# Native products of 8 columns ahead of streams, and odd heads of the scan on the other half of the rows

## The chip, the cores and the metric

The kernel runs on one core of one Trainium2 chip. The metric is the device time of one execution in microseconds (us); shorter is better. One program covers the whole computation: two layers of a network on 256 tokens of width 2048, in f32. The engines are named as in the profile: PE (TensorE, the matrix products), PEld (PE's weight loads), DVE (VectorE), ACT (ScalarE), POOL (GpSimd) and SP (SyncE, which here only issues transfers); ACTq is the queue on which ACT issues instructions such as transfers.

## What is computed

Layer 0 has differential attention as its mixer, layer 1 an RWKV-7 time mix; each is followed by an FFN. Cut to what the change touches:

```python
def sqrelu_mlp(h, w1, w2):                 # w1: 2048 x 8192, w2: 8192 x 2048
    u = jax.nn.relu(h @ w1)
    return (u * u) @ w2

# diff_attention: q = h @ wq, k = h @ wk, v = h @ wv, ..., o @ wo   (each 2048 x 2048)

def rwkv7_time_mix(h, ...):                # r = xr @ wr, k = xk @ wk, v = xv @ wv
    def step(state, inp):                  # 32 heads, state 64 x 64 each, 256 steps
        rt, wt, kt, vt, kkt, at = inp
        sa = jnp.einsum('bhvk,bhk->bhv', state, -kkt)
        state = (state * wt[:, :, None, :]
                 + sa[..., None] * (kkt * at)[:, :, None, :]
                 + vt[..., None] * kt[:, :, None, :])
        yt = jnp.einsum('bhvk,bhk->bhv', state, rt)
        return state, yt
    _, y = lax.scan(step, state0, xs)
    ...
    return out @ wo
```

## The kernel before

**Products.** A weight arrives as f32 (`raw`, loaded by SP's queue) and is split in two parts of a shorter float format: `whi` (a cast on ACT, L115) and `wlo` (a subtraction on DVE, L116). The other operand is split in the same way. Each product is made of three: high by high, high by low, low by high. In the form of `mm_a` (L220 to L222) the split weights are what 512 columns of the other side are multiplied with; in `mm_bh` (L254 to L256) the moving side has 256 columns. `proj_b` runs `mm_b` over panels: a panel is 256 output columns, its two accumulators are in PSUM banks of the role "mm" or "a" in turn, and one panel is 2 x 2 x 2 calls of `mm_bh` of 4 x 3 products, that is 96.

**FFN.** Each FFN runs four blocks (`fb`), which take 32 panels of the first weight as `proj_b` in a stream of 256-column products, each block followed by a stretch of 512-column products of the second weight (`mm_a`). The first block has only 6 panels in `proj_b`, since its first two are interleaved with the work ahead; the others have 8, that is 768 products. In front of the first product of blocks 1 to 3 stands a lead, chosen by the table LEADS (L33): native f32 products of the identity by itself into a bank of the role "d", of 128, 8, 24 or 72 columns, or four of 128. In FFN1's block 2 the entry is "low": the first three products stand in another order, and no native one is put there. A product of two f32 operands, called native here, leaves two records in the trace.

**Scan.** The time mix is computed in chunks of 64 tokens for four groups of eight heads (`g`). `scan_chain` works through one group: it loads the 64 x 64 inverses `TP` (in 32-blocks, and the off-diagonal parts `T1` and `T2` that make the missing block in ps1 and ps2) from DRAM, copies v into `VU`, transposes KB into `kbt` (L1275, L1277), and then goes through four chunks `c`, in each of which `W` is copied out of PSUM (L1330), eight heads' products `pu` of 64 x 64 x 64 are made from TP and W (L1339), and copied to `VU` (L1341). All eight heads' TP of a chunk stand on the same 64 rows (partitions), `b`. The generators of the groups and of the gates, norms and projections that surround them are merged to one stream by `beside`, `tick` and `yield` (a number says how much of other work is to come between); PE's order is fixed when the program is built, with products of the v and wo weights (`mm_a`, L220 to L222) as what stands between the steps of the scan. The semaphores among engines are set by the builder. Transfers of ACT and SP signal on eight shared completion lanes (DMAHW0 to DMAHW7 in the order below).

**Places in the profile.** wq and wk run to 187 us, wv, attention and wo to 390, FFN0 to 1104, the projections of the time mix to 1400, the scan to about 1680, FFN1 to 2400.

Of the kernel before, what the change touches and what calls it, by code (L numbers as in the profile page):

```python
# [20 lines left out]
P = 128  # L21
# [9 lines left out]


LEADS = {(0, 1): 128, (0, 2): 8, (0, 3): 24, (1, 1): 72, (1, 2): "low", (1, 3): 4}  # L33
# [4 lines left out]
class Kern:  # L38
    def __init__(self, ctx, tc, a, upto):
# [29 lines left out]
        self.lead = None  # L69
# [163 lines left out]

    def mm_bh(self, ps, XH, XL, half, c, m, first, last, ks=range(4)):
# [3 lines left out]
        for k in ks:  # L238
            xh, xl = XH[c][:, k, :], XL[c][:, k, :]
            lead, self.lead = self.lead, None  # L240
            if lead == "low":
                nc.tensor.matmul(ps[m], lhsT=wl[:, k, cl], rhs=xh, start=True, stop=False)
                nc.tensor.matmul(ps[m], lhsT=wh[:, k, cl], rhs=xh, start=False, stop=False)
                e = nc.tensor.matmul(ps[m], lhsT=wh[:, k, cl], rhs=xl, start=False, stop=False)
                continue
            else:
                if lead:
                    bank = self.ps("d")
                    with self.behind(self.done):
                        for _ in range(4 if lead == 4 else 1):  # L250
                            n = P if lead == 4 else lead
                            e = nc.tensor.matmul(bank[:, :n], lhsT=self.ident, rhs=self.ident[:, :n], start=True, stop=True)
                with self.behind(*([e] if lead else [])):
                    nc.tensor.matmul(ps[m], lhsT=wh[:, k, cl], rhs=xh, start=first and k == 0, stop=False)  # L254
# [4 lines left out]
    def proj_b(self, w, XH, XL, evac, panels=range(8), roles=("mm",)):  # L259
# [170 lines left out]
    def attention(self, xs):  # L430
        nc, a, tc = self.nc, self.a, self.tc
        with ExitStack() as ctx:
# [80 lines left out]
            self.proj_b(a["wq"], XH, XL, ev_q, range(1, 8), ["mm", "a"])  # L513
# [97 lines left out]
    def ffn(self, i, xs, fin, store=None):  # L611
# [3 lines left out]
        with ExitStack() as ctx:  # L615
# [42 lines left out]
            for fb in range(4):  # L658
# [16 lines left out]
                self.lead = LEADS.get((i, fb))  # L675
                self.proj_b(w1, XH, XL, evac, range(fb * 8 + 2 * (fb == 0), fb * 8 + 8), ["mm", "a"])
# [566 lines left out]
    def scan_chain(self, g, sp, pre, v, norm, done):  # L1243
# [54 lines left out]
        for b in (64, 0):  # L1298
            nc.scalar.copy(TP[b:b + 32, :, :, 32:64], ps2[b:b + 32])
# [261 lines left out]
```

## Time and profile before

| | before |
|---|---|
| time, three runs | 2404.79, 2409.40, 2412.78 us; median 2409.4 |
| profiled execution | 2411.38 us |
| its span on the core | 2409.6 us |
| PE busy | 2371.7 us, 98% |
| DVE, ACT, POOL busy | 1586.3 (66%), 1140.2 (47%), 152.1 (6%) |
| mean granted clock of PE | 0.995 |

The profile comes from one execution, whose own time stands beside its span: 1.8 us lie around it. Sums of the prediction are made against 2411.38. PE's busy time counts overlapping matmul records once; the end of a matmul is modelled, so the pitch between starts tells more than the length of a record. "xN" at the end of a row counts records; the two of a native product count as two. In the views by windows, a number after the window's bounds is its length, and the last of the engines' columns is followed by the granted clock of PE, 1.00 at 2.4 GHz and 0.50 at 1.2 GHz.

### The profile page before, as it was taken

How to read it: one execution, taken by the hardware profiler on the slowest of the kernel's cores; microseconds unless marked ns; L12 is line 12 of the kernel's file. 1: busy time of each engine (PE TensorE's matmuls, PEld its weight loads, DVE VectorE, ACT ScalarE, POOL GpSimd, SP SyncE). 2: the span in 40 equal slices, each digit the busy share in tenths (PEclk: the TensorE clock that was granted, in tenths of full speed). 3: DMA queues.
4: the chain of work that ended last, by engine and by line, in shares of the span. 5: the costliest groups of instructions: out<-in, count | busy, mean ns of one | idle time of the engine just before them, and what ended most of it. 6: DMA issues, size and time to landing. Idle time of an engine off the chain costs nothing. (4 is left out here: it accounts for less than half of the span.)

```text
span 2409.6 us, 42367 instructions
## 1 busy us (share of the span) xinstructions
PE 2371.7 (98%) x17166; PEld 2151.6 (89%) x17166; DVE 1586.3 (66%) x2543; ACT 1140.2 (47%) x1625; POOL 152.1 (6%) x208
## 2 busy tenths in 40 slices
PE   8999999999999999999999999999999999999997
PEld 8998888989989989988999977878998998988986
DVE  6667988745655655668779965668754655655655
ACT  6434656444434434455356544554644443443443
POOL 1000000000000000000001254311000000000001
PEclk9999999999999999999999999999999999999999
DMA  8665455655555555564556773435555555555563
GB/s 289 206 202 182 144 167 173 197 194 194 193 195 193 193 192 193 193 200 142 193 182 213 252 233 122 148 95 201 184 188 195 193 193 192 188 189 191 194 199 133
DMA packets 140851, 453.00 MB, mean 188 GB/s; under 512 B 27536, under 2 KB 27792, under 8 KB 140656
## 3 DMA queue, kind: packets, MB, share of 16 engines
q1 hardware_dynamic: 120176, 424.46, 53.4%
q0 software_dynamic: 5568, 16.52, 1.9%
q10 hardware_dynamic: 14912, 9.32, 1.3%
q8 instruction: 134, 2.20, 0.4%
q14 instruction: 61, 0.50, 0.1%
HBM read 433.99 MB, written 15.20 MB: 186 GB/s over the span
## 5 line engine op out<-in xcount | busy, mean ns | idle before, releaser
L116 DVE TENSOR_TENSOR wlo<-raw,whi 128x1024 fp32r<-128x1024 f32 (+1 forms) x772 | 945.0, 1228 | 598.5 <-ACT whi L115 572.3
L115 ACT CAST whi<-raw 128x1024 fp32r<-128x1024 f32 (+1 forms) x776 | 811.1, 1048 | 674.2 <-PE ps_mm L222 219.8
L254 PE MATMUL ps_mm<-fxh,whi 128*128 128x256 f32 x1023 | 284.7, 279 | 0.0
L255 PE MATMUL ps_mm<-fxl,whi 128*128 128x256 f32 x1023 | 283.9, 278 | 0.0
L256 PE MATMUL ps_a<-fxh,wlo 128*128 128x256 f32 x1024 | 283.7, 277 | 0.0
L254 PE MATMUL ps_a<-fxh,whi 128*128 128x256 f32 x1024 | 283.7, 277 | 0.0
L255 PE MATMUL ps_a<-fxl,whi 128*128 128x256 f32 x1024 | 283.7, 277 | 0.0
L256 PE MATMUL ps_mm<-fxh,wlo 128*128 128x256 f32 x1023 | 283.5, 277 | 0.0
L221 PE MATMUL ps_mm<-wlo,uh 128*128 128x512 f32 (+1 forms) x544 | 208.3, 383 | 0.0
L222 PE MATMUL ps_mm<-whi,ul 128*128 128x512 f32 (+1 forms) x544 | 208.3, 383 | 0.0
L220 PE MATMUL ps_mm<-whi,uh 128*128 128x512 f32 (+1 forms) x544 | 208.2, 383 | 0.0
L221 PE MATMUL ps_a<-wlo,uh 128*128 128x512 f32 (+1 forms) x512 | 196.0, 383 | 0.0
L222 PE MATMUL ps_a<-whi,ul 128*128 128x512 f32 (+1 forms) x512 | 195.7, 382 | 0.0
L220 PE MATMUL ps_a<-whi,uh 128*128 128x512 f32 (+1 forms) x512 | 195.5, 382 | 0.0
L256 PEld LDWEIGHTS ps_a<-fxh,wlo 128*128 128x128 f32 x1024 | 192.7, 188 | 0.0
L256 PEld LDWEIGHTS ps_mm<-fxh,wlo 128*128 128x128 f32 x1023 | 192.6, 188 | 0.0
L254 PEld LDWEIGHTS ps_a<-fxh,whi 128*128 128x128 f32 x1024 | 192.6, 188 | 0.0
L254 PEld LDWEIGHTS ps_mm<-fxh,whi 128*128 128x128 f32 x1023 | 192.4, 188 | 0.1
L255 PEld LDWEIGHTS ps_a<-fxl,whi 128*128 128x128 f32 x1024 | 192.2, 188 | 0.0
L255 PEld LDWEIGHTS ps_mm<-fxl,whi 128*128 128x128 f32 x1023 | 192.1, 188 | 0.0
L669 ACT CAST uh<-r 128x256 fp32r<-128x256 f32 x128 | 51.9, 406 | 269.0 <-DVE r L668 269.0
L222 PEld LDWEIGHTS ps_mm<-whi,ul 128*128 128x128 f32 x544 | 102.2, 188 | 19.8
(419 smaller groups left out, 4668.9 us busy)
## 6 DMA issues: line engine op xcount, KB each, us to landing
raw<-in_ffn SPq DMA_DIRECT2D x512, 512.0 KB, 4.3
raw<-in_wk SPq DMA_DIRECT2D x32, 512.0 KB, 5.0
raw<-in_wv SPq DMA_DIRECT2D x32, 512.0 KB, 4.2
raw<-in_wo SPq DMA_DIRECT2D x32, 512.0 KB, 4.3
raw<-in_rwr SPq DMA_DIRECT2D x32, 512.0 KB, 4.7
raw<-in_rwk SPq DMA_DIRECT2D x32, 512.0 KB, 4.5
raw<-in_rwv SPq DMA_DIRECT2D x32, 512.0 KB, 4.8
raw<-in_rwo SPq DMA_DIRECT2D x32, 512.0 KB, 4.5
```

The source lines that it names most:

```text
L115: self.nc.scalar.copy(hi[:, x], src[:, x])
L116: (eng or self.nc.vector).tensor_tensor(lo[:, x], src[:, x], hi[:, x].bitcast(F32), op=ALU.subtract)
L220: nc.tensor.matmul(ps[t][:, x], lhsT=xh, rhs=wh[:, k, :], start=st, stop=False)
L221: nc.tensor.matmul(ps[t][:, x], lhsT=xh, rhs=wl[:, k, :], start=False, stop=False)
L222: e = nc.tensor.matmul(ps[t][:, x], lhsT=xl, rhs=wh[:, k, :], start=False, stop=sp)
L254: nc.tensor.matmul(ps[m], lhsT=wh[:, k, cl], rhs=xh, start=first and k == 0, stop=False)
L255: nc.tensor.matmul(ps[m], lhsT=wh[:, k, cl], rhs=xl, start=False, stop=False)
L256: e = nc.tensor.matmul(ps[m], lhsT=wl[:, k, cl], rhs=xh, start=False, stop=last and k == 3)
L669: nc.scalar.copy(UH[-1][:, m % 4, :], r)
```

## The change

**Kicks.** The table LEADS goes. A method `kick()` gives, once for each panel that is named to it, one native product of the identity by 8 columns of itself, into a bank of the role "d", ordered behind `self.done`, the last product of the unit before; the panel's first product is ordered behind it. `proj_b` takes a list `kicks` of panels and sets `self.done` for each unit. Kicks stand ahead of: panel 3 of wq; panel 3 of rwr; in each FFN panel 3 of block 0 (the second of the six there) and the first panel of blocks 1, 2 and 3. That makes ten.

**Scan.** For odd heads, TP, W and so the operands of `pu` stand on the other 64 rows than for even heads (`b1 = 64 - b`). The copies of W (L1330) and VU (L1341) become two each (`swap`), of four heads; the two copies from ps2 to TP become eight of 32 x 4 x 32 elements; the loads of TP go from four of 32 x 16 x 32 to sixteen of 32 x 4 x 32, and a tile T2, on the buffer that SD uses later, takes four more loads, so that ps2's products read odd heads' blocks on the rows where T1 stands.

```diff
-LEADS = {(0, 1): 128, (0, 2): 8, (0, 3): 24, (1, 1): 72, (1, 2): "low", (1, 3): 4}
...
+    def kick(self):
+        if not self.due:
+            return []
+        self.due = False
+        with self.behind(self.done):
+            return [self.nc.tensor.matmul(self.ps("d")[:, :8], lhsT=self.ident, rhs=self.ident[:, :8], start=True, stop=True)]
...  (mm_bh)
-            lead, self.lead = self.lead, None
-            if lead == "low":
-                nc.tensor.matmul(ps[m], lhsT=wl[:, k, cl], rhs=xh, start=True, stop=False)
-                ...
+            with self.behind(*self.kick()):
+                nc.tensor.matmul(ps[m], lhsT=wh[:, k, cl], rhs=xh, start=first and k == 0, stop=False)
...  (proj_b)
         for pn in panels:
+            self.due = pn in kicks
...
-                self.mm_b(ps, XH, XL, self.unit(w[pn, u]), 8 * u, u == 0, u == 1)
+                self.done = self.mm_b(ps, XH, XL, self.unit(w[pn, u]), 8 * u, u == 0, u == 1)
...
-            self.proj_b(a["wq"], XH, XL, ev_q, range(1, 8), ["mm", "a"])
+            self.proj_b(a["wq"], XH, XL, ev_q, range(1, 8), ["mm", "a"], [3])
-                self.proj_b(w1, XH, XL, evac, range(fb * 8 + 2 * (fb == 0), fb * 8 + 8), ["mm", "a"])
+                self.proj_b(w1, XH, XL, evac, range(fb * 8 + 2 * (fb == 0), fb * 8 + 8), ["mm", "a"],
+                            [fb * 8 + 3 * (fb == 0)])
-                self.proj_b(a["rwr"], MH, ML, ev_r, [2, 3], ["mm", "a"])
+                self.proj_b(a["rwr"], MH, ML, ev_r, [2, 3], ["mm", "a"], [3])
...  (scan_chain)
+        T2 = sp.tile([P, 4, 2, 32], F32, name="T2", tag="SD")
...
             for blk in (1, 0):
-                dst = TP[b + 32 * blk:b + 32 * blk + 32].rearrange("s h a i -> s (h a) i")[:, :, 32 * blk:32 * blk + 32]
-                nc.scalar.dma_start(dst, self.ttd[g // 2][64 * blk + r0:64 * blk + r0 + 31:2].rearrange("r s i -> s r i"))
+                for e in range(2):
+                    b1 = (64 - b if e else b) + 32 * blk
+                    for q in range(2):
+                        dst = TP[b1:b1 + 32, 4 * q + 2 * e:4 * q + 2 * e + 2].rearrange("s h a i -> s (h a) i")
+                        r1 = 64 * blk + r0 + 16 * q + 8 * e
+                        src = self.ttd[g // 2][r1:r1 + 7:2].rearrange("r s i -> s r i")
+                        nc.scalar.dma_start(dst[:, :, 32 * blk:32 * blk + 32], src)
+                        if e and blk:
+                            nc.scalar.dma_start(T2[b + 32:b + 64, 2 * q:2 * q + 2].rearrange("s h a i -> s (h a) i"), src)
...
         for b in (64, 0):
-            nc.scalar.copy(TP[b:b + 32, :, :, 32:64], ps2[b:b + 32])
+            for e in range(2):
+                b1 = 64 - b if e else b
+                x, y = (z.rearrange("p (q e i) a j -> p q e (i a) j", q=2, e=2)[:, :, e] for z in (TP, ps2))
+                for q in range(2):
+                    nc.scalar.copy(x[b1:b1 + 32, q, :, 32:64], y[b:b + 32, q])
...
+        def swap(dst, src, b, back=False):
+            for e in range(2):
+                bs, bd = b, 64 - b if e else b
+                if back:
+                    bs, bd = bd, bs
+                x, y = (z.rearrange("p (h e x) -> p h e x", e=2, x=64) for z in (dst, src))
+                nc.scalar.copy(x[bd:bd + 64, :, e, :], y[bs:bs + 64, :, e, :])
...
-            nc.scalar.copy(W[b:b + 64, :], wps[b:b + 64, :])
+            swap(W, wps, b)
...
             for h in range(8):
-                nc.tensor.matmul(pu[b:b + 64, h * 64:(h + 1) * 64], lhsT=TP[b:b + 64, hx(h), t, :],
-                                 rhs=W[b:b + 64, h * 64:(h + 1) * 64], start=True, stop=True)
-            nc.scalar.copy(VU[b:b + 64, c, :], pu[b:b + 64, :])
+                b1 = 64 - b if h % 2 else b
+                nc.tensor.matmul(pu[b1:b1 + 64, h * 64:(h + 1) * 64], lhsT=TP[b1:b1 + 64, hx(h), t, :],
+                                 rhs=W[b1:b1 + 64, h * 64:(h + 1) * 64], start=True, stop=True)
+            swap(VU[:, c, :], pu, b, True)
```

The change moves instructions at two places that the prediction speaks of. The first is PE's order where block 2 of FFN1 begins; ps_a and ps_mm are PSUM banks by role, `uh` and `ul` the split inner activations, `fxh` and `fxl` the split input of the FFN. Before:

```order
L220 MATMUL ps_a<-whi,uh 128x512
L221 MATMUL ps_a<-wlo,uh 128x512
L222 MATMUL ps_a<-whi,ul 128x512
L242 MATMUL ps_mm<-fxh_18225,wlo 128x256
L243 MATMUL ps_mm<-fxh_18225,whi 128x256
L244 MATMUL ps_mm<-fxl_18229,whi 128x256
L254 MATMUL ps_mm<-fxh_18225,whi 128x256
L255 MATMUL ps_mm<-fxl_18229,whi 128x256
L256 MATMUL ps_mm<-fxh_18225,wlo 128x256
```

And now:

```order
L218 MATMUL ps_a<-whi,uh 128x512
L219 MATMUL ps_a<-wlo,uh 128x512
L220 MATMUL ps_a<-whi,ul 128x512
L238 MATMUL ps_d<-ident 128x8
L247 MATMUL ps_mm<-fxh_18355,whi 128x256
L248 MATMUL ps_mm<-fxl_18359,whi 128x256
L249 MATMUL ps_mm<-fxh_18355,wlo 128x256
```

The natural order of the three products is back, behind one native product of 8 columns (L238).

The second is ACT's order at the loads of group 2 of the scan; TP, T (T1, T2) are loaded from ttd and tnd, `o` is the normed output, `racc` an accumulator of wo, `kbt` a transposed KB. A number at the end counts equal rows behind one another. Before:

```order
L1266 DMA TP<-ttd_11366 32x16x32 x2
L1262 DMA T_16628<-tnd_11368 32x16x32
L1266 DMA TP<-ttd_11366 32x16x32 x2
L1269 COPY VU<-v 64x512 x4
L1418 ACTIVATE o<-ps_d,vec 128x128 x4
L314 COPY racc_16551<-ps_a 128x512 x2
L115 CAST whi<-raw 128x1024
L1277 COPY kbt<-ps_d 128x384
```

And now:

```order
L113 CAST whi<-raw 128x1024 x2
L1268 DMA TP<-ttd_11370 32x4x32 x8
L1258 DMA T_16696<-tnd_11372 32x16x32
L1268 DMA TP<-ttd_11370 32x4x32 x8
L1273 COPY VU<-v 64x512 x4
L1439 ACTIVATE o<-ps_d,vec 128x128 x4
L308 COPY racc_16619<-ps_a 128x512 x2
L113 CAST whi<-raw 128x1024
L1281 COPY kbt<-ps_d 128x384
```

Five loads ahead of the copies of v into VU (four of TP, one of T1) have become sixteen of a quarter of the size and one of T1, in a row; the copies behind them stand in the same order as before. With what each of the first of these loads waits for:

```order
L1268 DMA TP<-ttd_11370 32x4x32 [waits DMAHW5_49]
L1268 DMA TP<-ttd_11370 32x4x32 [waits DMAHW6_49]
L1268 DMA TP<-ttd_11370 32x4x32 [waits DMAHW0_49]
L1268 DMA TP<-ttd_11370 32x4x32 [waits DMAHW1_49]
L1268 DMA TP<-ttd_11370 32x4x32 [waits DMAHW2_49]
L1268 DMA TP<-ttd_11370 32x4x32 [waits DMAHW4_49]
L1268 DMA TP<-ttd_11370 32x4x32 [waits DMAHW5_49]
L1268 DMA TP<-ttd_11370 32x4x32 [waits DMAHW6_49]
L1258 DMA T_16696<-tnd_11372 32x16x32 [waits DMAHW7_49]
```

Each waits for one of the eight completion lanes.

## Rows read from the trace of the kernel before

**Rows 1.** The page's first part: busy us (share of the span) and instructions by engine.

```profile
PE 2371.7 (98%) x17166; PEld 2151.6 (89%) x17166; DVE 1586.3 (66%) x2543; ACT 1140.2 (47%) x1625; POOL 152.1 (6%) x208
```

**Rows 2.** Windows, records of L254 alone: length, PE busy, PEld busy, granted clock, DMA share, GB/s.

```profile
422.39:487.90 65.51, 53.20 (x192) 36.01 (x192) 1.00 0.61 197
...
749.51:836.64 87.13, 70.74 (x256) 48.02 (x256) 1.00 0.59 194
...
1711.85:1779.87 68.02, 54.12 (x192) 36.80 (x192) 1.00 0.59 193
...
2041.29:2131.75 90.46, 71.66 (x255) 47.86 (x255) 1.00 0.56 188
```

**Rows 3.** Timeline of PE ahead of three streams: start, us, engine, line, operation [idle before].

```profile
749.37 0.28 PE L252 MATMUL ps_d<-ident 128*128 128x8 f32 x2
749.51 0.36 PE L254 MATMUL ps_mm<-fxh,whi 128*128 128x256 f32 x1
749.71 0.28 PE L255 MATMUL ps_mm<-fxl,whi 128*128 128x256 f32 x1
...
1711.59 0.51 PE L294 MATMUL ps_b<-ident,pre_y 128*128 128x128 f32 x2
...
2218.79 1.05 PE L252 MATMUL ps_d<-ident 128*128 128x128 f32 x8
2219.59 0.36 PE L254 MATMUL ps_mm<-fxh,whi 128*128 128x256 f32 x1
```

**Rows 4.** Windows, records of L254 alone, in the RWKV projections (columns as in rows 2).

```profile
1262.54:1271.02 8.48, 6.74 (x24) 4.49 (x24) 1.00 0.41 134
1271.37:1272.84 1.47, 1.20 (x4) 0.73 (x4) 1.00 0.74 223
```

**Rows 5.** Windows of the scan: length, busy us of PE, PEld, DVE, ACT, POOL, granted clock, DMA.

```profile
1346.63:1347.71 1.08, 1.08 (x34) 1.01 (x33) 0.70 (x6) 1.08 (x3) 0.00 (x0) 1.00 1.03 421
1400.00:1680.00 280.00, 274.51 (x2778) 219.70 (x2777) 187.34 (x330) 140.50 (x222) 92.14 (x111) 0.99 0.48 153
1434.38:1435.45 1.07, 1.07 (x17) 1.00 (x16) 0.62 (x2) 0.90 (x1) 0.99 (x2) 1.00 0.00 0
1465.00:1472.50 7.50, 7.50 (x50) 6.55 (x48) 2.47 (x3) 1.28 (x3) 6.89 (x12) 0.59 0.58 166
```

**Rows 6.** Timeline of ACT and its queue (ACTq), then of PE, at group 2's loads.

```profile
1530.38 0.87 ACTq L1266 DMA_DIRECT2D TP<-ttd  x2
...
1533.21 2.51 ACT L1269 COPY VU<-v 64x512 f32<-64x512 f32 x4
1535.73 1.51 ACT L1418 ACTIVATE o<-ps_d,vec 128x128 f32<-128x128 f32 x4
...
1539.73 0.48 ACT L1277 COPY kbt<-ps_d 128x384 f32<-128x384 f32 x1
...
1539.15 0.55 PE L1275 MATMUL ps_d<-ident,kb 128*128 128x128 f32 x3
```

**Rows 7.** The line that loads TP (L1266): issue ns min/median/max, and landing.

```profile
L1266 ACTq DMA_DIRECT2D TP<-ttd x16: 310/501/1150, 1414.0 to 1585.0; - x16
...
DMA to landing us min/median/max: 2.1/3.6/6.7
```

**Rows 8.** Timelines at group 0's loads: ACT's queue, then PE.

```profile
1414.03 0.85 ACTq L1266 DMA_DIRECT2D TP<-ttd  x2
...
1422.87 0.50 PE L220 MATMUL ps_a<-whi,mh 128*128 128x512 f32 x1
```

**Rows 9.** Timelines in group 3: ACT, then PE.

```profile
1602.41 1.17 ACT L1299 COPY TP<-ps_mm 32x512 f32<-32x512 f32 x2
...
1604.28 0.88 PE L1339 MATMUL ps_mm<-W,TP 64*64 64x64 f32 x12 [0.23 <-issue]
```

**Rows 10.** Timeline of ACT in group 1.

```profile
1490.04 0.48 ACT L1277 COPY kbt<-ps_d 128x384 f32<-128x384 f32 x1 [3.91 <-PE ps_d L1275]
```

**Rows 11.** Timeline of PE in the scan, at the longest of its waits there.

```profile
1462.62 0.32 PE L1328 MATMUL ps_mm<-SB,ar 128*64 128x128 f32 x1 [1.60 <-DVE SB L1356]
```

More of the change, by code (lines that the diff above doesn't have):

```diff
@@ L68, in __init__ @@
         self.side = []
-        self.lead = None
+        self.done, self.due = None, False
         nc.scalar.activation(self.small(1, "act"), self.ones[:, 0:1], AF.Exp)
@@ L239, in mm_bh @@
             xh, xl = XH[c][:, k, :], XL[c][:, k, :]
-            lead, self.lead = self.lead, None
-            if lead == "low":
-                nc.tensor.matmul(ps[m], lhsT=wl[:, k, cl], rhs=xh, start=True, stop=False)
[L243 to L254, printed above, removed]
+            with self.behind(*self.kick()):
+                nc.tensor.matmul(ps[m], lhsT=wh[:, k, cl], rhs=xh, start=first and k == 0, stop=False)
             nc.tensor.matmul(ps[m], lhsT=wh[:, k, cl], rhs=xl, start=False, stop=False)
@@ L257, in mm_bh, with proj_b @@
         return e
-    def proj_b(self, w, XH, XL, evac, panels=range(8), roles=("mm",)):
+    def proj_b(self, w, XH, XL, evac, panels=range(8), roles=("mm",), kicks=()):
         for pn in panels:
+            self.due = pn in kicks
             ps = [self.ps(roles[pn % len(roles)])[:, :S] for _ in range(2)]
             for u in range(2):
-                self.mm_b(ps, XH, XL, self.unit(w[pn, u]), 8 * u, u == 0, u == 1)
+                self.done = self.mm_b(ps, XH, XL, self.unit(w[pn, u]), 8 * u, u == 0, u == 1)
             for m in range(2):
@@ L674, in ffn @@
                         evac(m, ps0[m])
-                self.lead = LEADS.get((i, fb))
-                self.proj_b(w1, XH, XL, evac, range(fb * 8 + 2 * (fb == 0), fb * 8 + 8), ["mm", "a"])
+                self.proj_b(w1, XH, XL, evac, range(fb * 8 + 2 * (fb == 0), fb * 8 + 8), ["mm", "a"],
+                            [fb * 8 + 3 * (fb == 0)])
                 if fb == 3:
@@ L1295, in scan_chain @@
                 for b in (64, 0):
-                    nc.tensor.matmul(ps2[b:b + 32, h, ap_, :], lhsT=T1[b + 32:b + 64, h, ap_, :],
-                                     rhs=TP[b + 32:b + 64, h, ap_, 32:64], start=True, stop=True)
-        for b in (64, 0):
-            nc.scalar.copy(TP[b:b + 32, :, :, 32:64], ps2[b:b + 32])
+                    r = slice(b + 32, b + 64)
+                    x = hx(h)
+                    nc.tensor.matmul(ps2[b:b + 32, x, ap_, :], lhsT=T1[r, x, ap_, :],
+                                     rhs=T2[r, x // 4 * 2 + x % 2, ap_, :] if h % 2 else TP[r, x, ap_, 32:64],
+                                     start=True, stop=True)
+        for b in (64, 0):
+            for e in range(2):
[3 more added lines that the diff above has]
+                    nc.scalar.copy(x[b1:b1 + 32, q, :, 32:64], y[b:b + 32, q])
         W = sp.tile([P, 512], F32, name="W", tag="W")
```

## The prediction

> **What bounds the kernel now.** I read the page first: TensorE is busy for 98% of the span [rows 1], so only what shortens PE's own work, or takes from or adds to its few waits, can move the end. Two kinds of PE time bear on this change. The first is the pace of the split products of 256 columns. One line's windows over eight FFN streams show it: the same 768 products take 87.13 us in one block and 90.46 in another, and the 576 of a first block 65.51 in one layer and 68.02 in the other [rows 2]. The reader is to see two paces at the full granted clock: 87.13/768 = 113.5 ns and 90.46/768 = 117.8 ns. What stands ahead of a stream goes with the pace. Ahead of a fast block stand two native records of 8 columns [rows 3]; block 2 of FFN1, the slow one, follows its last 512-column product with no native. In the slow first block of FFN1 the records ahead are two natives as well, but spread over 1711.85 - 1711.59 = 0.26 us instead of 0.14 [rows 3]. In the RWKV projections a slow stretch of 72 products (8.48 us) turns into a fast one behind four natives: 12 products in 1.47 us, of which 0.09 is the first one's longer pitch, hence (1.47 - 0.09)/12 = 115 ns, nearer to the fast pace [rows 4]; the same happens at seven such places.
>
> The second kind is the scan. From 1400 to 1680 us PE is busy 274.5 of 280 us and ACT 140.5 [rows 5]: PE is the bound there as well, and ACT has room on the average, but not at each place.
>
> **The kicks.** Ten single products of 8 columns (two records each) are put ahead of panels, and the leads of before go. One costs 749.51 - 749.37 = 0.14 us [rows 3]. Behind a 512-column stream the first product has a longer pitch anyway; inside a running 256-column stream I add that too, 0.20 instead of 0.11 [rows 3], hence 0.23 us.
> - FFN1 block 2: 90.46 goes to 87.13, less 0.14: -3.2 us. This is the pair of streams for which the trace has the exact precedent (8 columns behind a 512-column stream, fast).
> - FFN1 block 3: its lead of four products of 128 takes 2219.59 - 2218.79 = 0.80 us [rows 3] and becomes 0.14: -0.7.
> - FFN1 block 0: 68.02 - 65.51 = 2.5 us over 576 products. The kick stands ahead of the second of six panels, so 5/6 of it may go: -2.1 + 0.23 = -1.9. It is put within a running stream, where no 8-column native has stood; the nearest rows are those of the four natives [rows 4], so I take it in full and keep 0 as the other end.
> - FFN0 block 0 and wq run at the fast pace already: +0.23 each, nothing to gain. If a native within a fast stream sets the slow pace, the loss is 4.4 ns for each product left, 480 x 4.4 = 2.1 us each. wr is mixed: 0, from -0.8 to +0.8 (192 products).
> - FFN0 blocks 1 to 3, FFN1 block 1: 128, 8, 24 and 72 columns become 8: under 0.2 together, none counted.
> Sum -3.2 - 0.7 - 1.9 + 0.2 + 0.2 = **-5.4 us**, from -7 to +0.6.
>
> **The scan, PE's gain.** In each of 16 turns, eight products of 64x64x64 (16 records) read one half of the rows, and take 1.07 us, as from 1434.38 [rows 5]. Elsewhere the same shape alternates the two halves: 32 records in 1.08 us from 1346.63 [rows 5]. By half of that, 0.54, a turn would save 0.53; with only 16 records the ends weigh more, so I take 0.61, and 0.46 x 16 = **-7.3 us**, from 0 to -8.5. (The Trainium skill, TensorEngine Tiling (Array Packing), section Restrictions and Gotchas, speaks against it: different row tiles write to different PSUM banks and cannot reach the same bank at once. The eight products write one bank, so by that rule the sum would be 7.3 worse. This trace disagrees: the 32 records of 1.08 us also write one bank from both halves.)
>
> **The scan, ACT's copies.** A copy of 512 columns takes 0.58, two of them 1.17 [rows 9], one of 384 0.48 [rows 6], so 0.8 ns an element and 0.17 fixed: 0.38 for 256, 0.28 for 128. W and VU in two pieces cost 2 x 0.38 - 0.58 = +0.18 each, 32 times; the copies into TP, eight for two, 8 x 0.28 - 1.17 = +1.0 a group, four times. That is some 10 us of ACT time under PE's other products, except where PE waits for the copy right away (group 3, below).
>
> **The scan, ACT's transfers.** Loads of TP and T1 go from 6 to 22 a group, all issued by ACT; 11 to 21 of them now stand in a row ahead of copies that PE waits for. An issue took 0.50 us at the median, 0.31 at least, and landed after 3.6 us (2.1 to 6.7) [rows 7]. The order shows nearly each waiting for one of eight completion lanes, which SP's weight loads use too: 3.6/8 = 0.45 us a transfer if lanes set the pace. I take a pitch p = 0.48, from 0.35 to 0.65. (SP's loads wait for the lanes as well; they run several tiles ahead of the casts, and PE's waits in the scan name no load, so they are priced at nothing; without that cover their delay would fall under the upper p.) T2's four loads wait for the buffer of SD, which the group before has read for the last time after its third turn, ahead of the blocks: nothing. A block of n delays what is queued behind it:
> - Group 2: 17 loads from 1530.4, then the VU copies (2.5), then the o activations (1.5) which free ps_d for the next products, at 1539.15 before [rows 6]. After: 1530.4 + 17 x 0.48 + 4.0 = 1542.6, PE waits 3.4, and 0.5 for the racc copy behind that: +3.9.
> - Group 0: 1414.0 + 20 x 0.48 + 0.6 = 1424.2 for the v copy that frees ps_a; PE's next panel began at 1422.87 [rows 8]: +1.4, and 0.3 for the TP copies.
> - Group 1: 11 loads more are 5.3 us; ACT sat idle for 3.91 ahead of the next copies that PE needs [rows 10], and PE has other products to go on with: +0.2, at most 1.4.
> - Group 3: W's copy ended at about 1604.2 and PE's products stood right behind, at 1604.28 [rows 9]. TP's copies (+1.0) and W's second piece (+0.2) are exposed, and 0.7 of the block of 11 behind the G copy: +1.9.
> Sum of the scan: -7.3 + 3.9 + 1.7 + 0.2 + 1.9 = **+0.4**. At p = 0.36 group 2 gives 1.9, group 0 0.3, group 1 nothing, group 3 1.4: -3.7. At 0.65, 6.8, 5.1, 1.0 and 4.9: +10.5.
>
> **The scan, the clock.** At 1462.6 PE had waited 1.60 us [rows 11], and in the 7.5 us from 1465 its granted clock was 0.59, that is mostly the lower level, 1.2 GHz [rows 5]: 7.5 x 0.41 = 3.1 us lost. A wait of 3.9 us in group 2 is longer, so I count one more such stretch at four fifths: **+2.5**, from 0 to +6 (two).
>
> **Sum.** -5.4 + 0.4 + 2.5 = -2.5 us on the profiled execution's 2411.4, that is 2408.9. The median of the runs shown is 2.0 lower (2409.4), so **2406.9, say 2407 us**.
>
> **The rivals.**
> - *Issues are cheap* (p = 0.36) and no stretch of low clock is added: -5.4 - 3.7 = -9.1, 2400. For it: the loads are a quarter of the size, and the shortest issue took 0.31. Against it: a large number in a row, on lanes that SP also uses.
> - *ACT's row of loads becomes the bound in the scan*, p = 0.65, and the two longest waits each take the clock down: -5.4 + 10.5 + 6.2 = +11.3, 2421. It is slower than before from p = 0.54 on, if one low stretch comes with it: each 0.01 of p is worth some 0.6 us. For it: the lane waits, landings up to 6.7 us. Against it: 3.6 at the median.
> - *Kicks don't do what they say*: a native within a running fast stream sets the slow pace, and doesn't mend a slow one. -3.2 - 0.7 + 2 x 2.3 = +0.7, and the scan as above: +3.6, 2413. For it: the slow first block of FFN1 has natives ahead of it too [rows 3]. Against it: those were spread, as the kick isn't, and the four of [rows 4] follow each other at once.
> - *Products of both halves do not overlap in one bank*: no gain of 7.3, 2414. Against it: the window of 1.08 us. (This is the skill's rule, above.)
>
> **How the numbers follow.** Forecast 0.46, cheap issues 0.31, ACT as the bound 0.12, kicks 0.08, no overlap 0.03. A measurement of this kernel can tell about 0.3%, 7 us: faster is under 2402.2, slower over 2416.6. Cheap issues fall under the first (with 0.01 of the forecast's own spread), ACT as the bound over the second (with 0.01), the rest between: 0.32, 0.55, 0.13. The range, 2397 to 2418, takes in cheap issues with 3 us for the ends of the kicks and the products, and ACT as the bound up to p of about 0.62.
>
> **What would show it.** Block 2 of FFN1 in 87.13 us and the last five panels of FFN1's block 0 at 113.5 ns show the kicks right. The eight products of a turn in 0.61 us show the overlap; 1.07 would refute it. The wait of PE at group 2 (some 3.4 us, at about 1540, behind an o activation), one of 1 us at group 0 before a v panel, and a window of granted clock near 0.6 behind the first show the price; ACT's queue in the block of 17 gives p. If PE's idle time in the scan is no more than before (280 - 274.5 = 5.5 us), the cheap case holds; if over 15, the dear one. A stream that was fast and is slow behind its kick would make the first part wrong.

## The result, and the profile after

| kernel | median, us | ratio to before (95% interval) |
|---|---|---|
| before | 2408.9 | |
| after | 2430.5 | 1.0087 (1.0073 to 1.0100) |

The change made the kernel 21 us slower; 2407 was forecast, from 2397 to 2418. The profiled execution of after has a span of 2433.1 us, 23.5 more than that of before. PE's row of the page, which answers to [rows 1], and the page's row on how long the weight loads of wo took to land (last number, us):

```profile
PE 2374.4 (98%) x17170; PEld 2149.7 (88%) x17170; DVE 1588.5 (65%) x2543; ACT 1145.1 (47%) x1681; POOL 149.3 (6%) x208
...
raw<-in_rwo SPq DMA_DIRECT2D x32, 512.0 KB, 4.5
```

PE is busy for 2.7 us more; the rest is idle time. By the places where the same products start, the span grew like this: FFN1 -5.8 us, FFN0's block 0 +2.4, the projections of the time mix and what lies ahead of them -2.1, wq +3.6 (its waits for loads, which differ from one execution to the next by as much in kernels that leave wq alone), and the scan, from its first KB by AR product to FFN1's first block, +25.3. Two windows of the scan, before and after (length, busy us of PE, PEld, DVE, ACT and POOL, granted clock, DMA):

```profile
1407.30:1711.59 304.29, 297.78 (x3008) 243.92 (x3007) 209.06 (x389) 157.56 (x258) 92.13 (x109) 0.99 0.47 151
```

```profile
1411.18:1740.74 329.56, 302.01 (x3007) 243.62 (x3007) 212.26 (x391) 164.16 (x314) 89.05 (x109) 0.96 0.44 141
1432.00:1439.00 7.00, 5.84 (x16) 4.58 (x17) 2.78 (x2) 4.30 (x7) 6.37 (x9) 0.53 0.29 86
1445.80:1446.34 0.54, 0.54 (x17) 0.54 (x16) 0.00 (x0) 0.54 (x1) 0.54 (x1) 1.00 0.06 23
1476.00:1479.60 3.60, 3.60 (x35) 3.21 (x35) 1.51 (x3) 1.68 (x5) 0.55 (x2) 0.53 0.84 242
1553.50:1566.50 13.00, 7.70 (x76) 6.11 (x71) 4.76 (x7) 10.16 (x19) 2.11 (x1) 0.61 0.20 58
1574.50:1582.00 7.50, 6.97 (x40) 4.92 (x40) 5.03 (x6) 5.35 (x10) 3.42 (x3) 0.54 0.16 49
```

The first row of each is the scan: 304.29 us went to 329.56, of which PE was idle for 6.5 before and for 27.5 after. The third row of after is eight products of a turn on both halves: 0.54 us where [rows 5] had 1.07. But the window of [rows 5] ends where the product behind the eight starts; measured so, the turn takes 0.61. The other four are the stretches of low clock (0.53 to 0.61; before had one such, of 7.5 us [rows 5]). Added up over windows of 1 us (in each, PE's busy time times the share of the clock that was not granted), time lost to the clock went from 3.4 to 10.5 us.

PE's waits in the scan (us in total, times, longest), where before had no single wait above the 1.60 us for SB [rows 11]:

```profile
PE ps_d L1279 <- ACT o L1439: 6.1, 2, 5.3
PE ps_mm L1348 <- DVE SB L1377: 5.5, 3, 3.3
PE ps_mm L1291 <- DMA T<-tnd: 5.3, 2, 2.8
PE ps_a L218 <- ACT v L950: 2.6, 1, 2.6
```

Three of these four are new, and all three stand behind ACT's row of loads. Group 0's row on ACT (start, us, operation), to be read beside [rows 8]:

```profile
1417.44 0.33 ACTq L1258 DMA_DIRECT2D T<-tnd  x1
1418.68 1.29 ACTq L1268 DMA_DIRECT2D TP<-ttd  x3
...
1421.71 5.17 ACTq L1268 DMA_DIRECT2D TP<-ttd  x4
1427.21 0.31 ACTq L1258 DMA_DIRECT2D T<-tnd  x1
...
1430.58 1.89 ACTq L1268 DMA_DIRECT2D TP<-ttd  x4
1432.52 1.07 ACT L950 COPY v<-ps_a 128x512 f32<-128x512 f32 x2 [15.11 <-DMA TP<-ttd]
```

22 loads took from 1417.44 to 1432.47, and only then could ACT copy v. Group 2's, beside [rows 6]:

```profile
1544.94 1.41 ACTq L1268 DMA_DIRECT2D TP<-ttd  x3
1551.04 0.31 ACTq L1258 DMA_DIRECT2D T<-tnd  x1
1551.39 3.88 ACTq L1268 DMA_DIRECT2D TP<-ttd  x8
1555.36 2.50 ACT L1273 COPY VU<-v 64x512 f32<-64x512 f32 x4 [9.43 <-DMA TP<-ttd]
1557.88 1.50 ACT L1439 ACTIVATE o<-ps_d,vec 128x128 f32<-128x128 f32 x4
```

PE in the same place:

```profile
1552.94 1.19 PE L1291 MATMUL ps_mm<-T,qt 32*32 32x32 f32 x62 [2.84 <-DMA T<-tnd]
1559.43 0.90 PE L1279 MATMUL ps_d<-ident,kb 128*128 128x128 f32 x3 [5.30 <-ACT o L1439]
```

The row of 17 began at 1542.41 and ended at 1555.27: 12.9 us, 0.76 a load, with nothing issued from 1546.35 to 1551.04. PE waited 2.84 us for T1's second load, which stands in the middle of that row, and 5.30 for the o activations behind it.

How long one issue took (ns min/median/max), and landing, beside [rows 7]:

```profile
L1268 ACTq DMA_DIRECT2D TP<-ttd x64: 309/443/1357, 1418.7 to 1618.8; - x64
...
DMA to landing us min/median/max: 1.6/1.8/7.0
```

The kicks, by windows of the products' first line alone, as in [rows 2]: FFN0's block 0 behind its kick, FFN1's block 0 behind its kick, FFN1's block 2.

```profile
437.32:493.94 56.62, 45.05 (x160) 30.70 (x160) 1.00 0.57 189
1752.63:1807.14 54.51, 44.26 (x160) 30.01 (x160) 1.00 0.58 195
2068.66:2155.79 87.13, 70.75 (x256) 48.03 (x256) 1.00 0.59 194
```

480 products took 56.62 us (118.0 ns each) in the first, which was fast ahead of the kick, and 54.51 (113.6 ns) in the second, which was slow ahead of it. Block 2 went from 90.46 to 87.13, as forecast.

### The profile page after: what moved, and what is told of

It is laid out like the page before. It is cut to its first block, busy times and chain, and to the rows that moved or that the text cites. A ratio compares the mean times of both kernels' runs of the same rounds, so it can differ in the third digit from the quotient of the medians.

```text
span 2433.1 us, 42510 instructions
## 1 busy us (share of the span) xinstructions
PE 2374.4 (98%) x17170; PEld 2149.7 (88%) x17170; DVE 1588.5 (65%) x2543; ACT 1145.1 (47%) x1681; POOL 149.3 (6%) x208
## 4 chain that ended last, share of the span: by engine, by line
PE 87%; DVE 6%; DMA 3%; ACT 2%; issue 1%; ACTq 1%; SPq 0%; DVEq 0%
PE ps_mm L247 8%; PE ps_mm L249 8%; PE ps_mm L248 8%; PE ps_mm L220 7%; PE ps_mm L218 7%; PE ps_mm L219 7%; PE ps_a L249 6%; PE ps_a L247 6%; PE ps_a L248 6%; PE ps_a L218 6%; PE ps_a L219 5%; PE ps_a L220 5%; DVE wlo L114 2%; DMA raw<-in_rwv 1%; PE ps_b L782 1%
```

## The experiments

Each was timed in turns with the kernel before on the same chip; ratios are to its runs there. Unless said otherwise, an experiment has the leads of before.

**All kicks, scan of before.**

```diff
-LEADS = {(0, 1): 128, ...
+    def kick(self):
...  (scan_chain as before)
```

> The ten kicks of the change, with the scan of before. Theory (an 8-column native inside a running 256-column stream turns the pace over, whichever it was): FFN1 -5.8 us as in the changed kernel (block 0 -1.9, block 2 -3.2, block 3 -0.7), FFN0 block 0 +2.4, wq +0.5 for its slow stretch and up to 3 more if the longer wait seen there in the changed kernel comes with it, wr -0.6: together -3.5 us, at most 0, so 2403 to 2407 beside 2409. Rival (the kicks are what made the changed kernel slow): +15 or more.

2411.7 us, ratio 1.0008 (0.9997 to 1.0020): no difference that can be told. The kicks neither gave the 3.5 us nor made the loss.

**The scan alone.**

```diff
-    def scan_chain(...)      (before)
+    def scan_chain(...)      (after)
...  (LEADS as before, no kick)
```

> The scan of the change, with the leads of before and no kick. Theory (the scan lost what the changed kernel lost, by its loads): +24 us, from +20 to +28, with the eight products of a turn in 0.54 us. Rival (the kicks lost it): -8 to 0.

2434.3 us, 1.0111 (1.0094 to 1.0127), +25 us. The loss is the scan's.

**The loads alone.** Heads, products and copies as before.

```diff
-                nc.scalar.dma_start(dst, ...)                          # 32x16x32
+                for e in range(2):
+                    for q in range(2):
+                        nc.scalar.dma_start(dst[:, :, ...], src)       # 32x4x32
+                        if e and blk:
+                            nc.scalar.dma_start(T2[...], src)
```

> The scan of before, with all heads on the rows where they stood and one copy each for W and VU, but its 6 loads a group cut into the 22 of the change (T2 is loaded too and is used from the same rows). Theory (ACT's rows of loads, which wait for completion lanes, are the loss; the products of both halves are a gain of 8.5): +25 to +33 us, since the loss stays and the gain is missing; ACT's queue again needs 10 us or more for a block of 17, and PE waits behind the VU and o copies in groups 0 and 2. Rival (the split copies and the swap are the loss): -1 to +5 us.

2430.3 us, 1.0088 (1.0075 to 1.0101): +21 us, a little under the range that was given for the loads as the cause, far from the rival. PE's new waits are there again without any product or copy changed:

```profile
PE ps_mm L1295 <- DMA T<-tnd: 6.5, 3, 3.3
PE ps_d L1283 <- ACT o L1427: 4.6, 1, 4.6
...
PE ps_a L220 <- ACT v L956: 2.0, 1, 2.0
```

**A kick ahead of every panel.**

```diff
-                            [fb * 8 + 3 * (fb == 0)])
+                            range(fb * 8 + 3 * (fb == 0), fb * 8 + 8))
```

> The kicks of the change and the scan of before, but in both FFNs a kick stands ahead of every panel of a block instead of the first alone (in block 0 from the second of six on). Theory (each kick inside a stream turns the pace over): panels of 96 products go 113.3, 117.8, 113.3, 117.8 ns and so on, in every block, so that blocks 1 to 3 take 87.13 + 4 x 96 x 4.4 ns + 7 x 0.23 = 90.4 us. Rival 1 (a kick inside a fast stream sets the slow pace for good): only the first panel of a block is fast. Rival 2 (a kick sets the fast pace, and it was something else that made FFN0's block 0 slow): all panels at 113.3.

One execution, 2434 us, 25 more than before. Its kicks and slow panels account for some 20 of them: five streams took 3.3 more each, the two first blocks 2.4 and 0.7; FFN1's block 2 was as slow in before. Four panels of FFN0's block 0, which was fast ahead of the first kick (windows of the first line alone):

```profile
439.78:451.17 11.39, 9.07 (x32) 6.11 (x32) 1.00 0.59 192
451.31:462.30 10.99, 8.92 (x32) 5.99 (x32) 1.00 0.57 189
462.44:473.83 11.39, 9.07 (x32) 6.11 (x32) 1.00 0.55 186
473.97:484.96 10.99, 8.92 (x32) 5.99 (x32) 1.00 0.55 185
```

11.39, 10.99, 11.39, 10.99 us for 96 products, and so on through the blocks: a kick inside a stream turns the pace over, whichever it was. Both rivals fall.

The next four tried to keep the gain.

**Kicks where they should gain.**

```diff
-            self.proj_b(a["wq"], ..., ["mm", "a"], [3])
+            self.proj_b(a["wq"], ..., ["mm", "a"])
...  (rwr likewise)
-                            [fb * 8 + 3 * (fb == 0)])
+                            [fb * 8 + 3 * (fb == 0)] if fb or i else [])
```

> The scan of before. Kicks only ahead of blocks 1 to 3 of both FFNs (behind 512-column streams) and ahead of FFN1's block 0, panel 3, where the stream ahead was slow in each profile so far; none in wq, wr and FFN0's block 0. Theory (a kick behind a 512-column stream always gives the fast pace, one inside a 256-column stream turns it over): FFN1 -5.4 (block 0 -1.9, block 2 -3.2, block 3 -0.7, the rest the pitch), nothing else: 2403 to 2405 beside 2409. Rival (the pace of a stream is nothing that the end can see): 2409.

2407.6 us, 0.9993 (0.9982 to 1.0005). FFN1 went as expected in the profiled execution, but the median hardly moved. The profiles of all kernels together give a likely reason: without a kick, FFN1's block 0 was slow in 6 of the 14 profiled executions and fast in 8, FFN0's slow in 4 of 16. A kick gains in a slow stream and loses in a fast one. That the timed executions differ in this way isn't shown, since each kernel was profiled once; and the 4 us that the other kicks should give lie within the interval.

**Twelve loads instead of 22.** Heads 4 to 7 stand on the other rows instead of the odd ones.

```diff
-                    for q in range(2):
-                        dst = TP[b1:b1 + 32, 4 * q + 2 * e:4 * q + 2 * e + 2]...
+                    dst = TP[b1:b1 + 32, 4 * e:4 * e + 4]...            # 32x8x32
...
-                b1 = 64 - b if h % 2 else b
+                b1 = 64 - b if h >= 4 else b                           # h in 0, 4, 1, 5, 2, 6, 3, 7
```

> The leads of before. The scan of the change, but heads 4 to 7 of a group stand on the other rows instead of the odd ones, so that the heads of a half are neighbours in DRAM: TP's loads are 8 of 32x8x32 instead of 16, T2's 2 instead of 4, 12 a group in all instead of 22; the copies into TP are 4 instead of 8; eight products of a turn still alternate the halves. Theory (the loss is the number of ACT's loads in a row): a block of about 10 ends in 5 us, ahead of what PE needs in group 2 by the rows of before; -8.5 for the products and 1 to 3 back for copies and T1: -7 to -3 us. If the loss were in the swap: +15 or more.

2415.9 us, 1.0025 (1.0012 to 1.0038), +6: three quarters of the loss are gone, but it is still no gain. Not all of that is the ten loads fewer: heads 4 to 7 instead of the odd ones make the copies fewer too, and two runs below that differ in this alone lie 5 us apart. PE waits for o (3.3 us) and T1 (1.7) still.

**The same with the kicks of the run ahead of it.**

```diff
...  (scan_chain with twelve loads, kicks only ahead of FFN blocks, none in FFN0's block 0)
```

> The scan with 12 loads a group together with the kicks only behind 512-column streams and in FFN1's block 0. Theory: the two sums add, -5.4 and -5: 2396 to 2402. Rival (what one gives the other takes): 2404 or more.

2416.1 us, 1.0029 (1.0017 to 1.0041): nothing of the kicks can be told here either.

**TP's and T2's loads on POOL.**

```diff
-                        nc.scalar.dma_start(dst[:, :, 32 * blk:32 * blk + 32], src)
+                        nc.gpsimd.dma_start(dst[:, :, 32 * blk:32 * blk + 32], src)
...  (T2 likewise; T1 stays)
```

> The leads of before and the scan of the change, but TP's and T2's 20 loads a group are issued by POOL instead of ACT (T1's two stay on ACT). Theory (what stands behind the loads on ACT's queue, and the lanes that they share with SP's weights, is the loss): PE's waits for the v copy in group 0 and for the o activation in group 2 are gone, -8 to +3 us, the upper end if POOL's own work for SD and o is now late. Rival (the split copies and the swap): +15 or more, with the same waits.

2413.9 us, 1.0021 (1.0007 to 1.0036), +5 instead of +25. The wait for v is gone, that for o down to 0.4 us; PE waits for TP and T2 themselves now, and still for SB:

```profile
PE ps_mm L1354 <- DVE SB L1383: 5.5, 3, 3.2
PE ps_mm L1308 <- DMA TP<-ttd: 2.5, 1, 2.5
PE ps_mm L1308 <- DMA T<-ttd: 2.0, 2, 1.6
```

**Alternating products with the loads of before.**

```diff
-        T2 = sp.tile(...)
...  (loads of TP as before; ps2 reads TP; W, VU and TP copied as in the change)
```

> The leads of before. The products of a turn alternate the halves and all copies are split as in the change, but the loads are the 6 of before, to the rows of before: the odd heads' inverses are not put on the other rows and T2 is left out, so these heads are computed with the wrong blocks. Theory (products of both halves gain 8.5, the loads alone lose): -6 to -3 us, some of the gain lost where PE then waits longer for SB, which DVE delivers in group 0 (2.2 us in before, 5 in the kernels with alternating products). Rival (the split copies in the recurrence cost what the products give): -1 to +3.

2412.8 us, 1.0009 (1.0001 to 1.0018). The rival's time: without any added load the alternating products, as the change does them, gain nothing. PE's waits for SB sum to 5.0 us, against 2.2 in before. (In the one profiled execution the scan is 1.5 us shorter than in before, so the time of all executions isn't seen there.)

**Only the split copies.**

```diff
-            nc.scalar.copy(W[b:b + 64, :], wps[b:b + 64, :])
+            halves(W, wps, b)                    # even heads, odd heads, same rows
...  (VU likewise; eight copies into TP)
```

> The scan of before, all heads on the same rows and 6 loads, but the copies of W and VU in two pieces each and the copies into TP in eight, without a change of rows. Theory (ACT has the room, except in group 3 and where PE waits for W): 0 to +3 us. Rival (the copies are a loss of their own): +5 or more.

2413.6 us, 1.0015 (1.0006 to 1.0024), +3.5, a little over what was expected.

**Kicks only behind 512-column streams.**

```diff
-                            [fb * 8 + 3 * (fb == 0)])
+                            [fb * 8] if fb else [])
...  (none in wq and rwr, scan_chain as before)
```

> The scan of before, kicks only ahead of blocks 1 to 3 of both FFNs, none inside a 256-column stream. Theory (only these are sure, since what the pace is within a first block is chance): block 2 of FFN1 -3.3, block 3 -0.7, so -3.9 us, with the first blocks fast or slow as they fall. Rival: no gain.

2408.1 us, 0.9989 (0.9979 to 0.9998), -2.7: the sure part of the kicks, with 3.9 inside its interval.

**Twelve loads, ten of them on POOL, and these kicks.**

```diff
-                    nc.scalar.dma_start(dst[:, :, ...], src)             # 32x8x32
+                    nc.gpsimd.dma_start(dst[:, :, ...], src)
...  (kicks as in the run ahead of it)
```

> 12 loads a group with heads 4 to 7 on the other rows, TP's and T2's ten issued by POOL, and kicks only ahead of blocks 1 to 3. Theory: the scan's waits for TP and T2 that POOL's 20 loads caused (4.5 us) are halved at least, the scan is -2 to +2 beside before, with -3.9 for the kicks: 2403 to 2408 beside 2409. Rival (SB's wait and the low clock behind it hold): +2 or more.

2401.1 us, 0.9964 (0.9953 to 0.9975): faster than before by 8.7 us, better than forecast, and than the change by some 29. Some 3 us of it lie neither in the scan nor in the kicks, but at the program's end (see the kernel before with TP's loads on POOL, below).

Two more runs asked what this one is made of.

**Its scan with the leads of before.**

```diff
+LEADS = {(0, 1): 128, ...
...  (no kick; scan_chain of the run ahead of it)
```

> The scan of the run before (heads 4 to 7 on the other rows, 12 loads a group, ten of them issued by POOL) with the leads of before. Theory: that run's -8.7 us of the median was -2.7 by the kicks ahead of blocks 1 to 3 and -6 by the scan: -8 to -4 us here. Rival (its gain was in the kicks and in chance of the pace within a first block): -3 to +1.

2401.8 us, 0.9970 (0.9956 to 0.9983): the new `scan_chain` is worth 7 us of it, but not all in the scan. In the profiled execution the scan is 2.0 us shorter than in before, the stretch behind PE's last product 3.1 (12.0 instead of 15.1), and FFN1's block 0, which happened to be fast, 2.4. The same scan was 7.7 us shorter than before's in the profile of the run before, so one profile doesn't tell its worth.

**KB's product of group 1 taken from DVE.**

```diff
-            (nc.gpsimd if g > 1 else nc.vector).tensor_tensor(x, x, pl...)
+            (nc.gpsimd if g > 0 else nc.vector).tensor_tensor(x, x, pl...)
```

> The kernel with ten loads a group on POOL and kicks ahead of blocks 1 to 3, but the products of KB by PL in group 1 are on POOL instead of DVE (in before one of 1.21 us stands on DVE ahead of the SB that PE waits for; groups 2 and 3 have them on POOL already). Theory (SB of group 0 waits for DVE's queue, which is busy without a pause ahead of it): the wait of 3.0 us there falls to 1.5 to 2.0, the sum of SB's waits from 5.3 to about 4, -1 us for the whole, against which POOL may be late with KB for group 1. Rival (SB waits for the products that it reads): 3.0 us stay.

2399.8 us, 0.9961 (0.9948 to 0.9974), which can't be told from the kernel without the edit. In that kernel the products which SB reads ended at 1458.7, and PE waited for SB up to 1464.48:

```profile
1458.03 0.69 PE L1367 MATMUL ps_mm<-VU,kbt 128*64 128x64 f32 x16
...
1464.48 0.32 PE L1343 MATMUL ps_mm<-SB,ar 128*64 128x128 f32 x1 [3.04 <-DVE SB L1372]
```

while DVE worked without a pause on other things, SB at the end of its queue:

```profile
1458.68 0.52 DVE L140 TENSOR_TENSOR gn_t<-gn_y 128x8 f32<-128x8 f32 x1
...
1460.47 1.21 DVE L114 TENSOR_TENSOR wlo<-raw,whi 128x1024 fp32r<-128x1024 f32 x1
1461.60 0.55 DVE L146 SCALAR_TENSOR_TENSOR gn_y<-gn_t,gn_y 128x8 f32<-128x8 f32 x1
1462.07 0.68 DVE L1226 TENSOR_TENSOR qt<-ps_d,tri 128x512 f32<-128x512 f32 x1
...
1462.75 0.68 DVE L1226 TENSOR_TENSOR qt<-ps_c,tri 128x512 f32<-128x512 f32 x1
...
1463.42 0.41 DVE L1372 TENSOR_TENSOR SB<-ps_mm,SD 64x256 f32<-64x256 f32 x1
```

With KB's product gone the wait is no shorter:

```profile
1474.78 0.32 PE L1343 MATMUL ps_mm<-SB,ar 128*64 128x128 f32 x1 [3.48 <-DVE SB L1372]
```

DVE was busy up to SB there as well: the last step of the group norm (0.69 us) had come ahead of SB, and two wlo took 1.5 and 1.6 us instead of 1.2. So SB waits in DVE's queue, as the rows show, but taking one product out didn't shorten it; my expectation missed.

The last three separate the two parts of the gain, and test one step of the loss.

**The kernel before, with TP's loads on POOL.**

```diff
-                nc.scalar.dma_start(dst, self.ttd...)
+                nc.gpsimd.dma_start(dst, self.ttd...)
```

> The kernel before in all but one thing: TP's four loads a group are issued by POOL instead of ACT (T1's two stay). It tells how much of the 7 to 9 us of the kernels with ten loads on POOL came from taking loads off ACT, and how much from the alternating products. Theory (before's loads hid behind other work, the products are the gain): -1.5 to +1.5. Rival (loads on ACT cost before as well): -4 or more.

2407.4 us, 0.9983 (0.9973 to 0.9994), about -4, the rival's time, but not for the rival's reason. In the profiled execution the scan is no shorter than in before (304.6 us against 304.3). What is shorter is the stretch behind PE's last product: 12.5 us instead of 15.1. There POOL's queue runs an instruction DRAIN, and in before the end of the program waits for it (ns min/median/max; before, then this kernel):

```profile
L1550 POOLq DRAIN  x3: 46/93/8500, 2400.1 to 2409.1; - x3
```

```profile
L1550 POOLq DRAIN  x3: 46/98/3848, 2403.3 to 2409.9; - x3
```

The longest of the three took 8.50 us in each of the 14 kernels in which POOL issues 82 transfers, 3.85 here with 98, 5.32 in the three with 122, and 7.61 with the 162 of the run with TP's and T2's loads on POOL. So every kernel here that moves loads to POOL ends sooner, by 1.1 to 3.1 us from PE's last product on, whatever it does for the scan. What sets the length, which doesn't grow with the number alone, stays open.

**Heads 4 to 7 on the other rows, the loads of before.**

```diff
-        T2 = sp.tile(...)
...  (loads of TP as before; copies and products as in the kernel with twelve loads)
```

> As the kernel with alternating products and the 6 loads of before, but heads 4 to 7 instead of the odd ones stand on the other rows (contiguous copies, four instead of eight into TP); these heads are computed with the wrong blocks and T2 is left out. Theory (the eight small copies into TP and the strided ones ate the gain of that kernel): -6 to -3. Rival (taking loads off ACT is what made the kernels with ten loads on POOL fast): 0 to +2, as there.

2408.5 us, 0.9989 (0.9979 to 0.9999), about -2.5, between the two theories, and 5 us better than the same with odd heads. The two differ in the copies (four into TP instead of eight, and contiguous ones) and in the order of the heads; which of these counts wasn't told apart.

**T1's loads first.**

```diff
         for par in range(2):
+            nc.scalar.dma_start(T1[b:b + 32]...)
+        for par in range(2):
-            nc.scalar.dma_start(T1[b:b + 32]...)
```

> The scan of the change with the leads of before, T1's two loads ahead of TP's in a group's row instead of one at its head and one in its middle. Theory (PE's wait of 5 to 7 us for T1 comes from the loads ahead of T1's second one): that wait goes, and +25 becomes +18 to +23, since the v and o copies still stand behind the row. Rival (T1 lands late whatever its place): +25.

2441.7 us, 1.0123 (1.0107 to 1.0138), about +30: no gain, and its interval overlaps that of the scan alone (+25). The wait for T1 is gone from the list (6.7 us in the scan alone), but those behind the same row of loads, 5.7 and 2.9 there, grew by more:

```profile
PE ps_d L1288 <- ACT o L1448: 11.3, 2, 9.2
PE ps_a L220 <- ACT v L956: 5.8, 1, 5.8
```

The scan of the profiled executions, from the first KB by AR product to FFN1's block 0, added up over windows of 1 us (the rest is the length less idle time and time lost to the clock):

| kernel | length | PE idle | lost to the clock | rest |
|---|---|---|---|---|
| before | 304.3 | 6.5 | 3.4 | 294.4 |
| after | 329.6 | 27.5 | 10.5 | 291.6 |
| loads alone | 322.8 | 21.7 | 6.6 | 294.5 |
| split copies alone | 304.5 | 6.2 | 0.0 | 298.3 |
| alternating, loads of before, odd heads | 302.8 | 9.5 | 1.7 | 291.6 |
| the same, heads 4 to 7 | 300.2 | 10.1 | 0.0 | 290.1 |
| heads 4 to 7, twelve loads on ACT | 309.4 | 15.8 | 5.1 | 288.4 |
| heads 4 to 7, ten of twelve on POOL | 302.3 | 11.3 | 6.4 | 284.6 |
| odd heads, 20 of 22 on POOL | 307.6 | 16.1 | 5.7 | 285.8 |
| before, TP's loads on POOL | 304.6 | 8.4 | 3.4 | 292.8 |

The loads on ACT bring idle time and low clock, and leave PE's own work as it was (294.5). The copies add 3.9 us to PE's busy time with the same products, which are short waits, I take it, that the records count as work; that was not shown apart.

## Why the prediction was wrong

**ACT's row of loads: the mechanism was named, its term was mis-sized. This is the step that failed most.** The rival in which it becomes the bound got 0.12. The pitch was taken as 0.48 us, from 0.35 to 0.65, and came out at 0.76 in group 2 and 0.68 in group 0. The issue itself was right: 0.44 at the median, and in the runs of equal loads one each 0.48 (eight from 1551.39 to 1555.27). What was missing are single long holds. Group 2's row stood still from 1546.35 to 1551.04, 4.7 of its 12.9 us. The load behind the hold waits for a completion lane, and by the trace's events that lane's last user was a weight load of SP, issued in this row (start, us, two loads):

```profile
1546.54 1.46 SPq L122 DMA_DIRECT2D raw<-in_rwo  x2
```

Such loads land after 4.5 us (page, above); this one landed at 1551.02, and ACT's load was issued at 1551.04. Group 0 had another kind: three of its four loads from 1421.71 on were issued by 1423.51, and the fourth only at 1426.57, when a load of the row itself, issued on that lane at 1419.52, had landed after 7.0 us. It goes the other way too: SP's next weight load waited for lanes that ACT's loads held (queue's waits, us in total, times, longest):

```profile
SPq L122 <- DMA TP<-ttd: 20.6, 3, 10.0
```

That side was priced at nothing, and rightly: PE's waits in the scan for a cast of these weights sum to 0.7 us.

My estimate of 3.6/8 = 0.45 us spread the landings evenly over the lanes; in order on one queue, one late lane stops all that stands behind it. With the measured 0.76 in its place, the prediction's formula for group 2 gives 1530.4 + 12.9 + 4.0 - 1539.15 + 0.5 = 8.6 us, and PE waited 2.84 + 5.30 = 8.1. In group 0, 22 loads took 15.0 us (0.68 each) and PE waited 2.45 for T1 and 2.60 for v. By the prediction's own rate, 0.6 us for each 0.01 of p, pitches of 0.68 to 0.76 put the scan at 0.4 + 12 to 0.4 + 16.8, an estimate beyond the range it was made for; with the 7.1 us of the clock that is 19.5 to 24.3 of the 25.3 measured. (The rival's +10.5 at p = 0.65 has a slip: group 3 by its own terms is 1.2 + 0.7 + 11 x 0.17 = 3.8 there, not 4.9.) That the loads are the cause is shown (the loads alone: +21 us; the same loads on POOL: +5). How much of it is lanes and how much the number of loads is read from the trace only: in group 2, 17 x 0.48 = 8.2 us are issue, 4.7 the hold.

**T1's place was not in the working,** though the order showed its load in the middle of the row. It made waits of its own (5.3 us in two) but, as far as the run with T1 first shows, no loss of its own: there the later waits are longer.

**The clock: right in kind, too small.** One more stretch of low clock was counted, 2.5 us; there were four against one, and the loss rose by 7.1. In before the low level came behind a wait of 1.60 us [rows 11]; the new waits are of 2.5 to 5.3 us. Such a wait doesn't always bring it: in the kernel with kicks only behind 512-column streams, whose scan is that of before, PE waited 1.6 us for SB as well and 1.9 for T1, and the profile has no low clock in the scan. Over the five profiles of before's scan the loss is 0 to 3.4 us while its length stays within 303.5 to 304.5, so the loss by the clock isn't all loss for the end, and part of the 7.1 may be chance.

**The products came as forecast: 0.61 us for eight up to the next product's start, instead of 1.07, though not in every turn.** (The Trainium skill's rule in TensorEngine Tiling (Array Packing), Restrictions and Gotchas, that different row tiles cannot use one PSUM bank at once, does not hold here: these products write one bank from both halves.) In the profile of after, twelve of the 16 turns went to half of what they took in before: 0.46 to 0.48 us instead of 0.92 from the first start to the last, and 0.81 instead of 1.65 in the one at the low clock. In the other four, other products stand among the eight in PE's order: three took 1.1 us and one 0.7. With the split copies alone four turns are parted too (1.5 us instead of 0.92). Over all 256 records of the scan's turns, from start to next start, PE's work fell by 6.8 us, near the 7.3 forecast, and not by the 8.5 that my expectations reckoned with from the 0.54. But that was not 6.8 us for the end. The split copies, priced at 1.2 us in group 3, 0.3 in group 0 and nothing in the others, cost 3.5 alone: W's and VU's second pieces stand in each turn's recurrence, 16 times, and the prediction hid them under PE's other products. And PE, being early, waited longer for SB (1.60 us at the longest before [rows 11], 3.04 in the fast kernel), which stands in DVE's queue. With the loads of before the alternating products came out 2 us slower, not 7 faster.

**The kicks.** Block 2 (-3.2) and block 3 (-0.7) of FFN1 came as worked out. The rival on the kicks was half right: a kick inside a fast stream does set the slow pace (FFN0's block 0 lost 2.4 us, priced at 2.3 there), but it mends a slow one as well (FFN1's block 0: -1.9, as forecast). It turns the pace over. The step that failed was to take the pace of the first blocks in one profiled execution for that of all. Up to FFN0's block 0 the 16 kernels without a kick there run the same instructions, and yet it was slow in 4 profiles and fast in 12: the order of instructions ahead of it doesn't settle the pace, so a kick there can't be counted on. Kicks only behind 512-column streams gave -2.7, all kicks +2 (not told from 0), against -5.4 forecast. The difference of some 4.6 us fits first blocks that were fast in most executions and were turned slow (2.3 each), with wq's slow stretch on top; the timed executions have no trace, so this isn't shown.

Together: -5.4, +0.4 and +2.5 were forecast. In the profiled execution of after all that lies outside the scan gave -1.8 (with the +3.6 of wq's waits in it), and the scan +25.3: idle +21.0, clock +7.1, rest -2.8.

## What to carry to other kernels

A row of loads on a compute engine's queue is priced by its slowest member: what holds one lane (here a 512 KB weight load of another queue, and once a load of the row itself that landed after 7.0 us) holds everything that stands behind it on the engine, so cut one load into four only where nothing that the bound engine needs stands behind, or issue them on an engine with nothing urgent. Look for a gain in the place where it should be: of what the loads on POOL gave, up to 3.1 us came at the program's end. A gain in a step of a recurrence counts only as far as the slowest of the step's engines: price the added copy at each turn, and look at what the bound engine will wait for when it is early. A pace seen in one execution is a property of the program only if other executions show it.

## What had not been expected

A native product of 8 columns inside a stream of 256-column products turns the stream's pace over between 113.3 and 117.8 ns, at the full granted clock, at every one of the places where one was put, in the FFNs, wq and wr (panels of 96 in 10.99 and 11.39 us by turns); behind a 512-column stream it gave the fast pace in each of the profiles. What in the engine this is stays open. And four loads a group of 64 KB each, moved from ACT's queue to POOL's with nothing else changed, gave about 4 us (0.9983, 0.9973 to 0.9994) though the profiled scan was no shorter: POOL's DRAIN at the program's end, 8.50 us in all kernels that leave POOL's transfers alone, took 3.85, and the program ended 2.7 us sooner after PE's last product.
